# Retention queries and keys by seven block products, and weight sums by accumulating loads

## The chip, the cores and the metric

The kernel runs on one core of a Trainium2 chip. The metric is device time in microseconds of one execution. TensorE multiplies, VectorE and ScalarE read the products out of the PSUM banks and prepare operands, GpSimd does masks and small powers, and the queue of SyncE issues the transfers between DRAM and on-chip memory.

## The reference

Two layers on a 1024 x 1024 input. Layer 0 is a retention of four heads; layer 1 is a stick-breaking attention of eight heads whose keys and values come from the output of layer 0. The change touches the projections of layer 0:

```
u = rms_norm(h, ret_norm_pre[i])
proj = u @ ret_w_in[i]
q, k, v, g = split(proj)            # per head: q, k of 256 columns, v, g of 512
q = rope(q, pos)                    # [x1 cos - x2 sin, x1 sin + x2 cos]
k = rope(k, pos) * 256 ** -0.5
o = retention_chunkwise(q, k, v)
o = (o - mean(o)) * rsqrt(var(o) + EPS)
o = o * silu(g)
y = o @ ret_w_out[i]
```

## The kernel before

The sequence is worked in two halves of 512 columns (t = 0, 1): retention of both halves (phases A0 and A1), then attention of both (C0 and C1). A retention phase goes through its four heads (u = 0 to 3), an attention phase through four pairs of heads.

**Numbers as two parts.** Every operand of a matmul is held as a rounded part and a remainder. `split` (L574) makes them: ScalarE writes the rounded part (L577, L580 with a scale), VectorE the difference (L578, L581). `mm3` (L412) then issues three matmuls per product (L415, L416, L417) into one PSUM bank.

**A head of the retention** has three stages on TensorE:

- *Queries and keys*, `AHead.qk` (L730) by `proj` (L457): four units of weights of 128 x 1024; four banks (two `ma`, two `mb`), each the output of one block of 128 columns of q or k, and 96 matmuls that stream 512 columns. When the last k-tiles are through, `rope` (L715, operations L717 to L722) turns two banks at a time with twelve VectorE operations and four splits over all, into the tile `qk`, of which there is one buffer.
- *The output of the head before*, `outproj` (L484): 16 chunks of 6 matmuls. Its sides are the scores of the new head, `scores` (L869), and statistics.
- *Values and gates*, `AHead.vg` (L770): seven block products instead of eight. Its quadrants are the two halves of the 512 time columns, the two halves of the 1024 inputs, and values against gates. The sums of inputs that it needs are made once per phase, by `sums` in `a_prep` (L630), and kept as `X.T`. The sums of weights are made by VectorE in `left` (L777): additions and subtractions at L797, L800, L803 and L806 on tiles `wraw` and `S`, then split into `whl`. The products go in the order 1, 2, 5, 6, 3, 7, 4, each in two units; products 6 and 7 add to the banks of 1, and 3 to those of 5. `copy` (L821, ScalarE) and `plus` (L825, VectorE) read partial results out, `vput` (L742) and `gput` (L746) finish values and gates.

The first head of A0 does it in another way (`first_v`, `qk`, `first_g`) and keeps that.

**What sets the order.** The program is emitted as chunks: `merge` (L524) weaves side steps into the chunks of a stage, each with a number of chunks to leave free at its start and end. `run` (L1531 to L1546 for the retention) says which sides go where: the rest of the mixing and the gate of the head before go into the query/key stage, the scores into the output stage, the first mixing steps into the value/gate stage. For the last head (u = 3) the first 4 of 16 output chunks go ahead of values and gates, and 12 after. Then `arrange` (L101) orders every engine's queue anew: from a duration for each instruction (`_time`, L68), the number of buffers of each tile (`BUFS`, L319) and a model of the DMA queue, it plans the program by latest start times five times over (`place`, `justify`) and fixes the order of each queue to that of the best plan.

**Buffers** that matter here: `whl` 3 (split weights), `wraw` 6 (raw weights, 128 x 512), `S` 2 (128 x 1024, the sums), `f2` 6, PSUM banks `ma`, `mb`, `z`, `o` 2 each. `raw_w` (L342) hands out `wraw` tiles, and in attention, by `rings`, also tiles of other names. All transfers are issued by SyncE through `dma` (L359).

## Time and profile before

| | |
|---|---|
| three runs | 1715.91, 1716.36, 3299.96 us; median 1716.36 |
| the profiled execution | 1716.91 us, span 1714.8 us |
| granted TensorE clock | 0.997 |
| instructions of TensorE | 8057 matmuls and as many weight loads |
| DMA | 348.78 MB, mean 203 GB/s |

The third run is a single slow execution. In the profile, `PE` is TensorE's matmuls and `PEld` its weight loads, `DVE` is VectorE, `ACT` ScalarE, `POOL` GpSimd, `SP` SyncE. A group of instructions is listed as its line, engine and operation, output tile and input tiles, shape and count, then busy microseconds and mean nanoseconds of one, then the idle time before it and what ended it. A row of the windows gives for each engine the busy time and the number of instructions, then the granted clock, the busy share of the DMA engines and their GB/s. A row of waits gives the waiting line, the releaser, the total, the count and the longest. A row of the chain gives start, length and what ran.

### The profile page before, as it was taken

To read this page: it belongs to the slowest core of one execution; us is meant where nothing else is said; L and a number is where in the kernel's file an instruction comes from. 1 tells how busy PE (TensorE), PEld (TensorE's weight loads), DVE (VectorE), ACT (ScalarE), POOL (GpSimd) and SP (SyncE) were. 2 spreads that over 40 slices of the span, in tenths; PEclk is the share of its full clock that TensorE was granted. 3 is DMA by queue.
4 is the path that set the end of the run, shared out by engine and by line. 5 is a ranking of instruction groups with operands and counts; after the bars stand their busy time and mean duration, and the time that the engine had idled before them with its cause. 6 is when DMAs were issued, how large, how long until landed. Compare 5 with 4: busy or idle time off the path is not lost.

```text
span 1714.8 us, 23975 instructions
## 1 busy us (share of the span) xinstructions
PE 1700.1 (99%) x8057; PEld 1419.0 (83%) x8057; DVE 1308.4 (76%) x2213; ACT 880.9 (51%) x1646; POOL 142.8 (8%) x275
## 2 busy tenths in 40 slices
PE   9999999999999999999999999999999999999997
PEld 7888888888888888878888888888888888888887
DVE  8856868889867978688888778667887756656865
ACT  6435536555545535355655544544674445445643
POOL 0000101010010000101010100000001001001001
PEclk9999999999999999999999999999999999999999
DMA  5236475668545676376896999667883763463523
GB/s 187 98 105 203 148 236 185 203 193 271 187 146 176 225 240 209 98 256 209 291 320 198 332 314 308 209 209 257 280 292 111 252 225 101 160 219 99 162 95 125
DMA packets 182250, 348.78 MB, mean 203 GB/s; under 512 B 20208, under 2 KB 24432, under 8 KB 182128
## 3 DMA queue, kind: packets, MB, share of 16 engines
q1 hardware_dynamic: 182128, 347.26, 61.0%
q8 instruction: 63, 1.03, 0.2%
q14 instruction: 59, 0.48, 0.1%
HBM read 273.78 MB, written 73.40 MB: 202 GB/s over the span
## 4 chain that ended last, share of the span: by engine, by line
PE 99%; DMA 0%; DVE 0%; ACT 0%; issue 0%; SPq 0%; POOL 0%; DVEq 0%
PE pmb L415 13%; PE pmb L417 13%; PE pmb L416 13%; PE pma L415 12%; PE pma L417 12%; PE pma L416 12%; PE po L417 5%; PE po L416 5%; PE po L415 5%; PE pz L1355 2%; PE pz L417 2%; PE pz L416 2%; PE pz L415 2%; PE pz L983 1%; PE pz L551 0%; DMA S<-in_xT_dram 0%
## 5 line engine op out<-in xcount | busy, mean ns | idle before, releaser
L577 ACT ACTIVATE whl<-wraw 128x512 fp32r<-128x512 f32 x323 | 190.8, 625 | 203.4 <-PE pmb L417 80.4
L578 DVE TENSOR_TENSOR whl<-wraw,whl 128x512 fp32r<-128x512 f32 x323 | 214.3, 686 | 64.3 <-ACT whl L577 63.1
L415 PE MATMUL pma<-xh,whl 128*128 128x512 f32 x384 | 153.1, 399 | 0.0
L415 PE MATMUL pmb<-xh,whl 128*128 128x512 f32 x384 | 152.4, 397 | 0.0
L417 PE MATMUL pma<-xh,whl 128*128 128x512 f32 x384 | 150.1, 391 | 0.0
L417 PE MATMUL pmb<-xh,whl 128*128 128x512 f32 x384 | 150.0, 391 | 0.0
L416 PE MATMUL pma<-xh,whl 128*128 128x512 f32 x384 | 149.9, 390 | 0.0
L416 PE MATMUL pmb<-xh,whl 128*128 128x512 f32 x384 | 149.6, 390 | 0.0
L1325 DVE TENSOR_TENSOR_SCAN sgn<-sgn 128x384 f32<-128x384 f32 (+4 forms) x64 | 86.5, 1354 | 27.7 <-POOL sgn L1323 27.7
L580 ACT ACTIVATE whl<-wraw,gn 128x256 fp32r<-128x256 f32 (+1 forms) x144 | 80.4, 600 | 50.0 <-PE pmb L417 32.4
L577 ACT ACTIVATE AT<-pz 128x512 fp32r<-128x512 f32 (+1 forms) x96 | 46.3, 487 | 108.0 <-PE pz L1355 105.9
L1322 POOL TENSOR_SCALAR_AFFINE_SELECT A<-A 128x128 f32<-128x128 f32 x64 | 33.1, 516 | 775.1 <-ACT A L1317 775.1
L578 DVE TENSOR_TENSOR AT<-pz,AT 128x512 fp32r<-128x512 f32 (+1 forms) x96 | 52.9, 555 | 57.6 <-ACT AT L577 57.1
L581 DVE SCALAR_TENSOR_TENSOR whl<-wraw,gn,whl 128x256 fp32r<-128x256 f32 (+1 forms) x144 | 82.0, 601 | 17.1 <-ACT whl L580 16.5
L415 PE MATMUL pmb<-oT,whl 128*128 128x512 f32 x240 | 94.9, 396 | 0.0
L417 PE MATMUL pmb<-oT,whl 128*128 128x512 f32 x240 | 93.8, 391 | 0.0
L416 PE MATMUL pmb<-oT,whl 128*128 128x512 f32 x240 | 93.7, 391 | 0.0
L577 ACT ACTIVATE whl<-S 128x512 fp32r<-128x512 f32 x104 | 63.0, 628 | 48.1 <-PE pmb L417 12.5
L417 PEld LDWEIGHTS pmb<-xh,whl 128*128 128x128 f32 x384 | 72.1, 188 | 15.8
L417 PEld LDWEIGHTS pma<-xh,whl 128*128 128x128 f32 x384 | 72.1, 188 | 15.6
L416 PEld LDWEIGHTS pmb<-xh,whl 128*128 128x128 f32 x384 | 72.2, 188 | 13.5
L415 PEld LDWEIGHTS pmb<-xh,whl 128*128 128x128 f32 x384 | 72.2, 188 | 13.4
(389 smaller groups left out, 4614.0 us busy)
## 6 DMA issues: line engine op xcount, KB each, us to landing
wraw<-in_wts_dram SPq DMA_DIRECT2D x522, 256.0 KB, 3.6
y<-f SPq DMA_DIRECT2D x120, 256.0 KB, 3.2
f<-y SPq DMA_DIRECT2D x88, 256.0 KB, 4.1
S<-in_wts_dram SPq DMA_DIRECT2D x44, 256.0 KB, 4.1
vo<-in_wts_dram SPq DMA_DIRECT2D x42, 256.0 KB, 4.3
ko<-in_wts_dram SPq DMA_DIRECT2D x40, 256.0 KB, 4.4
T<-AT SPq DMA_DIRECT2D x32, 256.0 KB, 4.7
sc<-T SPq DMA_DIRECT2D x16, 512.0 KB, 5.1
```

Source lines behind the costliest of these rows:

```text
L415: MM(p, lh, rh, start=start, stop=False, **kw)
L416: MM(p, lh, rl, start=False, stop=False, **kw)
L417: MM(p, ll, rh, start=False, stop=stop, **kw)
L577: A_.activation(dst[0], src, AF.Copy)
L578: V.tensor_tensor(dst[1], src, f32(dst[0]), ALU.subtract)
L580: A_.activation(dst[0], src, AF.Copy, scale=scale)
L581: V.scalar_tensor_tensor(dst[1], src, scale, f32(dst[0]), ALU.mult, ALU.subtract)
L983: nc.tensor.transpose(pt[:, 128 * e:128 * e + 128], on[:, 128 * e:128 * e + 128], ident[:])
L1322: first = G.affine_select(a[:, dg], a[:, dg], [[-1, 128]], ALU.is_gt, 0.0, base=0, channel_multiplier=1)
L1325: V.tensor_tensor_scan(n[:, :W][:, ::-1], n[:, :W][:, ::-1], n[:, :W][:, ::-1], 1.0, ALU.mult, ALU.bypass)
L1355: nc.tensor.transpose(p[:, 128 * tb:128 * tb + 128], self.A[hh][tb][:, c0:c0 + 128], ident[:])
```

## The change

1. Queries and keys of all heads but the first of A0 are made by seven block products too. Quadrants are the two time halves of 256 columns, the two halves of the inputs, and q against k. A product has 24 matmuls that stream 256 columns, its two blocks of 128 output columns side by side in one bank. Block b of a product's bank is the b-th 128 columns of q (`m` 0) or of k (`m` 1), so the four `put`s each rotate one time half of q or of k: q's second half after product 2, k's first after 7, k's second after 4, q's first after 3. The weights are laid out in quadrants on the host (`_quads`), and a copy for the first head is appended.
2. Sums of weights, for queries and keys and for values and gates, are no longer made by VectorE: a second transfer, issued by GpSimd, adds into the tile that the first filled. Where a difference was needed, the signs of the sums of inputs and of the gate are turned, and `outproj` subtracts.
3. Values and gates go in the order 5, 1, 2, 6, 7, 3, 4.
4. `wraw` has 4 buffers for 6, `S` 3 for 2. For the last head 8 output chunks go ahead of values and gates instead of 4, and their banks are the usual ones.
5. The planner knows transfers of GpSimd, and orders reads of one bank by two engines.

```
-    BUFS = dict(xh=8, tab=2, wraw=6, whl=3, S=2, ...
+    BUFS = dict(xh=8, tab=2, wraw=4, whl=3, S=3, ...
...
+    def plus_dma(dst, src):
+        nc.gpsimd.dma_start(dst, src, accum_op=ALU.add)
...
-            V.tensor_tensor(a[:, 0], q[0], q[1], ALU.subtract)
-            V.tensor_tensor(a[:, 1], q[2], a[:, 0], ALU.subtract)
+            V.tensor_tensor(a[:, 0], q[1], q[0], ALU.subtract)
+            V.scalar_tensor_tensor(a[:, 1], a[:, 0], -1.0, q[2], ALU.mult, ALU.subtract)
...
+        def qk7(self):
+            X, quads = self.X, self.base if self.h else 128
+            box = {}
+            order = (1, 2, 5, 6, 7, 4, 3)
+            def left(n):
+                w = S("whl", [2, 1024], F32R)
+                if n == 5:
+                    box["S"] = S("S", [1024])
+                for j in range(2):
+                    cl = slice(512 * j, 512 * j + 512)
+                    src = box["S"][:, cl] if n in (5, 6, 3) else raw_w()
+                    b11, b12, b21, b22 = [wts[quads + i, :, cl] for i in range(4)]
+                    parts = {1: (b11,), 2: (b21,), 5: (b12, b22), 6: (b11,), 3: (b21,), 7: (b11, b12), 4: (b22,)}[n]
+                    for i, b in enumerate(parts):
+                        (dma if i == 0 and n not in (6, 3) else plus_dma)(src, b)
+                    split((w[:, 0, cl], w[:, 1, cl]), src)
+                return w
...
+            def put(m, half, p, c):
+                if (m, half) == (0, 1):
+                    q = self.qkt = S("qk", [4, 2, 512], F32R)
+                    self.q, self.k = [q[:, 0], q[:, 1]], [q[:, 2], q[:, 3]]
+                tl = slice(256 * half, 256 * half + 256)
+                cos, sin = [z[:, tl].unsqueeze(1).broadcast_to([128, 2, 256]) for z in (X.cos, X.sin)]
+                V.tensor_tensor(c[:], p[:], c[:], ALU.add)
+                x = c[:].rearrange("p (b t) -> p b t", b=2)
+                r, y = S("f2", [2, 256]), S("f2", [2, 256])
+                V.tensor_tensor(r[:], x, cos, ALU.mult)
+                V.tensor_tensor(y[:], x, sin, ALU.mult)
+                if m:
+                    V.tensor_tensor(r[:, 0], y[:, 1], r[:, 0], ALU.subtract)
+                    V.scalar_tensor_tensor(r[:, 1], r[:, 1], -1.0, y[:, 0], ALU.mult, ALU.subtract)
+                else:
+                    V.tensor_tensor(r[:, 0], r[:, 0], y[:, 1], ALU.subtract)
+                    V.tensor_tensor(r[:, 1], r[:, 1], y[:, 0], ALU.add)
+                res = self.qkt[:, 2 * m:2 * m + 2]
+                split((res[:, :, 0, tl], res[:, :, 1, tl]), r[:])
...
+            def chunk(n, kt):
...
+                    first = {1: "ma", 2: "ma", 5: "mb", 4: "mb"}.get(n)
+                    if first:
+                        box["p", n] = PS(first)
+                w, p = box["w"], box["p", {6: 1, 7: 1, 3: 5}.get(n, n)]
+                fresh = n in (1, 2, 5, 4)
+                xh, xl = right(n, kt)
+                for b in range(2):
+                    nl = slice(256 * kt + 128 * b, 256 * kt + 128 * b + 128)
+                    mm3(p[:, 256 * b:256 * b + 256], w[:, 0, nl], w[:, 1, nl], xh, xl, fresh and kt == b == 0, kt == 3, goes_on=not fresh or b == 1)
+                if kt < 3:
+                    return
+                if n in (1, 5, 6, 7):
+                    box[n] = copy(p)
+                if n == 2:
+                    put(0, 1, p, box[1])
+                elif n == 3:
+                    put(0, 0, p, box[6])
+                elif n == 7:
+                    put(1, 0, p, box[5])
+                elif n == 4:
+                    put(1, 1, p, box[7])
...
                     elif n == 5:
-                        a, b, src = load(1, i), load(1, 2 + i), s
-                        V.tensor_tensor(src, a, b, ALU.add)
+                        dma(src, at(1, i))
+                        plus_dma(src, at(1, 2 + i))
                     elif n == 6:
-                        a, src = load(0, i), s
-                        V.tensor_tensor(src, src, a, ALU.subtract)
+                        plus_dma(src, at(0, i))
                     elif n == 3:
-                        src = load(0, 2 + i)
-                        V.tensor_tensor(src, src, s, ALU.subtract)
+                        plus_dma(src, at(0, 2 + i))
                     elif n == 7:
-                        a, src = load(1, 2 + i), s
-                        V.tensor_tensor(src, a, src, ALU.subtract)
+                        dma(src, at(0, i))
+                        plus_dma(src, at(1, i))
...
-            order = [(n, i) for n in (1, 2, 5, 6, 3, 7, 4) for i in range(2)]
+            order = [(n, i) for n in (5, 1, 2, 6, 7, 3, 4) for i in range(2)]
...
-                        first = {1: "ma", 2: "o", 5: "mb", 4: "mb"}.get(n)
+                        first = {5: "ma", 1: "mb", 2: "o", 4: "mb"}.get(n)
...
-                        held = last.out(yd, None, None if u < 3 else ("ma",) * 4)
-                        go(held if u < 3 else held[:4],
+                        held = last.out(yd, None, None if u < 3 else None)
+                        go(held if u < 3 else held[:8],
```

In the planner, a transfer holds the queue of its issuer for 400 ns (SyncE) or 1100 ns (GpSimd) and lands 1550 or 3100 ns after its turn on the rings.

More of the change, by code (lines that the diff above doesn't have):

```diff
@@ L119, in arrange @@
         for name, m in reads:
-            s.before |= {o.k for o, n, w in last[name] if w and n & m}
+            s.before |= {o.k for o, n, w in last[name] if n & m and (w or name in banks and o.eng != s.eng)}
             s.behind |= set([o.k for o, n, w in last[name] if not w and n & m and o.eng == s.eng][-1:])
@@ L137, in arrange @@
         s.busy, s.whole = _time(s, chip)
-        s.shares = s.eng == "Pool" or s.eng == "DVE" and sum(b.tensor.name not in banks for b in s.ins) > 1
+        s.shares = s.eng == "Pool" and not s.moves or s.eng == "DVE" and sum(b.tensor.name not in banks for b in s.ins) > 1
         steps.append(s)
@@ L202, in justify @@
         line = taken[s.eng]
-        busy = max(s.busy, 400.0) if s.eng == "SP" else s.busy
+        busy = HOLD[s.eng] if s.moves else s.busy
         i = bisect.bisect(line, (t, t))
@@ L276, in place @@
         busy, whole = s.busy, s.whole
-        if e == "SP":
-            ring_free = max(t + 1000.0, ring_free) + busy * 1.05
-            end, busy = ring_free + 1550.0, 400.0
+        if s.moves:
+            ring_free = max(t + 600.0 + HOLD[e], ring_free) + busy * 1.05
+            end, busy = ring_free + (3100.0 if e == "Pool" else 1550.0), HOLD[e]
         else:
@@ L482, in proj, with outproj @@
         return Chunks([lambda j=j: chunk(j) for j in range(16)], lambda: get(0))
-    def outproj(base, oT, y_d, first, acc=None, tags=None):
+    def outproj(base, oT, y_d, first, acc=None, tags=None, turned=lambda: False):
         box = {}
@@ L1636 @@
                   _out_units(so[b:b + 512])]
+    units.append(_quads(np.concatenate([wi[:, 0:256], wi[:, 1024:1280]], axis=1)))
     gains = np.stack([np.asarray(g).reshape(8, 128) for g in
```

69 lines of the change are left out of this document (46 added, 23 removed).

## The prediction

> **What bounds the kernel now.** I read the page first, then the waits of TensorE, then the chain of waits in narrow windows, for the spacing of matmuls.
>
> ```profile
> span 1714.8 us, 23975 instructions
> PE 1700.1 (99%) x8057; PEld 1419.0 (83%) x8057; DVE 1308.4 (76%) x2213; ACT 880.9 (51%) x1646; POOL 142.8 (8%) x275
> PE 99%; DMA 0%; DVE 0%; ACT 0%; issue 0%; SPq 0%; POOL 0%; DVEq 0%
> q1 hardware_dynamic: 182128, 347.26, 61.0%
> ```
>
> The chain that ended last is TensorE for 99% of the span. Its waits by releaser, all of them over the execution:
>
> ```profile
> PE pz L415 <- ACT qk L577: 1.8, 1, 1.8
> PE pz L388 <- DVE f L386: 1.7, 1, 1.7
> PE pma L415 <- ACT oT L580: 1.2, 1, 1.2
> PE pz L1464 <- POOL col L1458: 1.0, 1, 1.0
> PE pz L1454 <- DVE acc L1447: 0.9, 1, 0.9
> ```
>
> Five waits, 6.6 us together; only the first lies in the part that changes. So the time is the number of matmuls times their spacing, and a gain comes from matmul columns alone: work taken off VectorE (76% busy) buys nothing by itself. The spacing is the distance between starts in the chain, not the duration in the list of groups, which overlaps its neighbours. A run of 128x512 matmuls, then the 128x256 matmuls of the last output projection:
>
> ```profile
> 99.96 0.23 PE pma L416
> ...
> 103.82 0.22 PE pz L983 x2
> ```
> ```profile
> 1689.91 0.12 PE pmb L417
> ...
> 1693.15 0.12 PE pma L417
> ```
>
> 17 steps in 3.86 us are 0.227 us each; 27 steps in 3.24 us are 0.120 us each. Half the columns cost 0.53 of the time.
>
> **The change part by part.** Seven query/key projections change form (heads 1 to 3 of the first half, all four of the second).
>
> *Matmuls.* Before, one takes 4 units x 2 x 4 blocks x 3 = 96 matmuls of 512 columns: 96 x 0.227 = 21.8 us. After, 7 products x 4 k-tiles x 2 blocks x 3 = 168 matmuls of 256 columns: 168 x 0.120 = 20.2 us. Saved 1.64 us each, **11.5 us** in all; one part in eight of the columns, less 72 more matmuls' fixed share. Values and gates keep their matmuls; only their order changes. By the Trainium skill (TensorE: Matmul & The Clock Gate, Back-to-back issue gap) a stream of load-and-multiply pairs runs at about 81 ns for 128 columns and 131 ns for 512; an estimate between them is 98 ns for 256, and by it the change would lose 3.9 us a projection, 27 us in all. This trace has 227 and 120 ns for the same things, so the sum goes by the rows.
>
> *The wait that goes.* The one wait in the changed part is that of the scores of the last head:
>
> ```profile
> 729.00:735.70 6.70, 4.88 (x18) 3.61 (x17) 6.70 (x12) 3.73 (x7) 0.00 (x0) 0.87 0.66 229
> 735.70:739.20 3.50, 3.50 (x13) 2.87 (x13) 1.51 (x3) 0.00 (x0) 0.41 (x1) 0.76 0.89 259
> ```
>
> TensorE lacks 1.82 us of the first stretch, and the granted clock falls to 0.87 and 0.76 in the two (0.13 x 6.7 + 0.24 x 3.5 = 1.7 us): 3.5 us. VectorE is full (6.70 of 6.70): it turns four blocks through the 12 rotary operations and 4 splits, all issued at the end. After the change three quarters of this lies earlier in the projection, and eight output chunks instead of four stand between it and the scores (4 x 6 x 0.227 = 5.4 us more cover). I take the whole **3.5 us** as gained; the ends are 0 and 3.5. What is late next is nothing on the list above.
>
> *VectorE and ScalarE.*
>
> ```profile
> L577 ACT ACTIVATE whl<-wraw 128x512 fp32r<-128x512 f32 x323 | 190.8, 625 | 203.4 <-PE pmb L417 80.4
> L578 DVE TENSOR_TENSOR whl<-wraw,whl 128x512 fp32r<-128x512 f32 x323 | 214.3, 686 | 64.3 <-ACT whl L577 63.1
> L797 DVE TENSOR_TENSOR S<-wraw,wraw 128x512 f32<-128x512 f32 x28 | 19.1, 686 | 11.7 <-DMA wraw<-in_wts_dram 11.6
> L825 DVE TENSOR_TENSOR f<-pmb,f 128x512 f32<-128x512 f32 x28 | 18.9, 683 | 1.3 <-PE pmb L417 1.3
> L722 DVE TENSOR_TENSOR f<-f,f 128x512 f32<-128x512 f32 x16 | 10.9, 680 | 0.0
> L578 DVE TENSOR_TENSOR AT<-pz,AT 128x256 fp32r<-128x256 f32 x16 | 6.7, 421 | 9.2 <-ACT AT L577 9.1
> L581 DVE SCALAR_TENSOR_TENSOR whl<-wraw,gn,whl 128x256 fp32r<-128x256 f32 x78 | 34.0, 479 | 4.4 <-ACT whl L580 4.4
> ```
> ```profile
> 183.70:212.00 28.30, 28.30 (x134) 23.45 (x133) 21.48 (x40) 14.09 (x25) 3.86 (x9) 1.00 0.47 159
> 212.00:246.00 34.00, 34.00 (x172) 28.61 (x171) 23.08 (x44) 11.97 (x22) 3.02 (x5) 1.00 0.63 212
> 246.00:286.20 40.20, 40.20 (x178) 33.30 (x178) 36.25 (x60) 25.96 (x45) 1.93 (x3) 1.00 0.64 207
> 592.70:623.80 31.10, 31.10 (x146) 25.78 (x146) 23.31 (x43) 10.70 (x18) 4.58 (x9) 1.00 0.59 202
> 623.80:649.50 25.70, 25.70 (x121) 21.62 (x121) 19.22 (x33) 8.56 (x16) 2.08 (x4) 1.00 0.69 236
> 649.50:693.20 43.70, 43.70 (x198) 36.27 (x197) 38.40 (x65) 26.53 (x47) 2.61 (x5) 1.00 0.62 199
> ```
>
> The six stretches are query/key, output and value/gate stage of a head of each half; the third number after PE and PEld is VectorE's. Value/gate loses 16 additions of 0.686: 11.0 us. Query/key gains 14 - 8 = 6 weight splits (4.1 us), and four puts of 0.68 + 2 x 0.68 + 0.42 + 0.48 + 0.69 = 3.63 (14.5 us) replace 16 operations of 0.68 (10.9 us): 7.7 us more. That stage then wants 21.5 + 7.7 = 29.2 us of VectorE in 28.3 - 1.6 = 26.7 us of TensorE (31.0 in 29.5 in the other half). The surplus of about 2 us is hidden if the last put may slip into the output stage, where VectorE has 10.9 and 6.5 us free and the scores come only after five chunks (6.8 us). I take **0**; uncovered it is 2 us x 7 = 14. ScalarE has half its time free everywhere. One wait is new: q and k have one buffer, and q's second half is put after product 2 of 7 rather than at the end, while in the second half of the sequence the head before still reads its own q in the mixing woven into this stage. The put's last two operations stand in ScalarE's and VectorE's queues until that mixing is through; the scores that need them come a stage later, so this too is 0, and without that room it is part of the 14.
>
> *The accumulating loads.* Per head 24 loads that add into a tile, issued by GpSimd, which the trace does not show. Nearest rows, a plain load and GpSimd's and SP's holds:
>
> ```profile
> S<-in_wts_dram SPq DMA_DIRECT2D x44, 256.0 KB, 4.1
> ```
> ```profile
> L555 POOL TENSOR_TENSOR col<-small,mhalf 128x4 f32<-128x4 f32 x8 | 11.3, 1408 | 110.5 <-DVE small L553 110.5
> ```
> ```profile
> L360 SPq DMA_DIRECT2D wraw<-in_wts_dram x10: 327/332/333, 1263.8 to 1278.9; - x10
> ```
>
> Landing: 4.1 us if adding is free, 8.2 if it costs a second load; issue: 0.33 to 1.41 us. They matter at one place: in the new projection product 6 follows 5, and 6's weights are 5's tile after the split and two accumulations. From the split of 5 to the weights of 6: issue, landing, two splits (2.0 us): 6.7 us at the low end, 1.41 x 2 + 8.2 + 2.0 = 13.0 at the high one. Three split buffers let 5 be split by some 2.6 us (two halves of 0.63 + 0.69) after product 1 starts, so TensorE has three products (3 x 24 x 0.120 = 8.6) less 2.6, plus the mixing woven in (21 x 0.227 = 4.8 in the first half, 33 x 0.227 = 7.5 in the second, none in its first head): 10.8, 13.5 and 6.0 us. Costs: 0.7 to 3 x 2.2 + 7.0 = 13.6 us. I take **1.5**, nearer the low end, since the row is that of a load into the same tile. Behind a waiting load on GpSimd stand the causal masks of the scores and the small powers of the normalisation; both feed work that is a chunk or more away from TensorE's need.
>
> *Products 6 and 7 on one bank.* ScalarE must copy product 6 before 7 adds to it.
>
> ```profile
> L821 ACT ACTIVATE f<-pma 128x512 f32<-128x512 f32 x42 | 24.7, 590 | 11.4 <-PE pma L417 11.1
> ```
> ```profile
> 1686.75 0.28 PE L416 MATMUL pma<-qk,xh 128*128 128x256 f32 x1
> ```
>
> Drain 0.28 - 0.12 and copy 0.59: 0.75 us, filled by product 4 or woven work where its weights are there; for values the other bank's three matmuls (0.68) fill nearly all. Ends 0 and 7 x 0.8 = 5.6; I take **1.5**, as woven work stands in most heads.
>
> *Load buffers 6 to 4.* The densest stage with this ring alone is the shared values of the last half:
>
> ```profile
> 1246.80:1278.70 31.90, 31.90 (x145) 26.56 (x144) 25.66 (x34) 24.47 (x46) 2.56 (x6) 1.00 0.92 302
> ```
> ```profile
> DMA to landing us min/median/max: 3.2/4.1/5.5
> ```
>
> 20 loads; a slot is held 0.33 + 4.1 + 1.4 = 5.9 us, so four slots pass 20 in 29.4 us of 31.9; with 1 us of waiting, 34.4. Ends 0 and 5; I take **1.0**.
>
> Signs carried through and the two half-width subtractions of the input sums cost nothing: they ride on operations that stay. **Sum**, against the profiled execution's own 1716.91 us (0.55 above the median): 1716.9 - 11.5 - 3.5 + 1.5 + 1.5 + 1.0 = **1705.9 us**, 0.64% less.
>
> **The rivals.**
> 1. *The accumulate chain shows* (13.0 us from split to weights): 1705.9 - 1.5 + 13.6 = 1718 us. For it: the first head of the second half has no cover. Against: 4.1 us for a load into this tile.
> 2. *VectorE becomes the bound of the query/key stage*, its put late and the scores waiting: 1705.9 + 14 = 1720 us. For it: 29.2 in 26.7, and the old wait was of this kind. Against: free time right behind, and a head as a whole loses 3.3 us of VectorE.
> 3. *Slower than before: the DMA engines become the bound of the retention.* A plain load's 128 packets take 0.61 x 1714.8 x 16 / 182128 = 92 ns each, 0.735 us of all 16 engines. A head's engines are busy 60 us in the first half (0.47 x 28.3 + 0.63 x 34 + 0.64 x 40.2) and 63 in the second; it loses 10 plain loads (7.4 us) and gets 24 accumulating ones. If one costs k plain ones, the need is 53.0 + 17.6k of 100.9 us, and 55.9 + 17.6k of 98.9. At k = 2 that is 0.88 and 0.92, the share at which the window above ran without a wait; it decides from k = 2.4. At k = 3: 5.1 us x 3 + 9.9 x 4 = 55 us, 1761 us. Against: an addition reads two operands and writes one, k near 2. The Trainium skill (Collectives: The Full Stack, The bandwidth ceiling) says the same: an adding transfer reads two sources and gets half the rate. No run here shows it yet.
> 4. *The narrow matmul does not keep 0.120 us* because weights bind:
>
> ```profile
> L417 PEld LDWEIGHTS pma<-qk,xh 128*128 128x128 f32 x21 | 4.0, 192 | 0.0
> ```
>
> A load lasts 192 ns there; if loads could not overlap, 7 x 168 x 0.072 = 85 us come on top, 1791 us, and the change would not do what it says. Against: those same loads ran at 0.120. This is the direction of the skill's spacing rule above.
>
> **How the numbers follow.** Forecast 0.68, rivals 0.12, 0.10, 0.08 and 0.02. With every new cost at zero the time is 1701.9; 1176 matmuls at 1 ns less give 1700, the low end. The high end takes in rivals 1 and 2 and a little of both: 1724. About 2% (34 us) is what a measurement of this kernel can tell from no change; slower by more is most of rivals 3 and 4 (0.07), faster by more none of the cases, as TensorE's columns do not give 34 us (0.01). Within 2%: 0.92.
>
> **What would show it.** Right: 168 matmuls a projection 0.120 us apart; no wait of the scores near the end of the second half's retention; TensorE's waits still under 12 us; VectorE's additions into S gone and its share down by some 20 us. Wrong: TensorE waiting for the copies or splits of query/key weights behind an accumulating load (rival 1), for the put of q and k (2), a DMA share above 0.9 through the retention with loads landing late (3), or spacing well above 0.120 (4).

## The result, and the profile after

The changed kernel takes 1764.16 us in the median (1763.45 to 1768.92), the kernel before 1715.91 beside it: a ratio of 1.0289, with a 95% interval of 1.0266 to 1.0312 (ratios are taken over the single executions, not from the two medians). Medians leave out one far slower execution each of the kernel before and of the experiments e9, e12 and e15; with it they are 1716.13, 1727.6, 1719.8 and 1712.0, and the expectations quoted below name e9 by its 1727.6. The changed kernel is 48 us slower, where 1705.9 with a range of 1700 to 1724 was forecast. The profiled execution took 1768.92 us, its span is 1767.2.

The page of the changed kernel, the lines that answer to those of before, and the one for the loads that GpSimd issues (median us to landing at its end):

```profile
span 1767.2 us, 25359 instructions
PE 1711.0 (97%) x8561; PEld 1444.9 (82%) x8561; DVE 1290.2 (73%) x2199; ACT 916.0 (52%) x1716; POOL 294.6 (17%) x443
q1 hardware_dynamic: 172048, 328.91, 55.7%
q0 software_dynamic: 24192, 44.05, 15.0%
PE 78%; DMA 10%; issue 5%; DVE 4%; ACT 2%; POOL 1%; SPq 0%; POOLq 0%; DVEq 0%; ACTq 0%
S<-in_wts_dram POOLq DMA_DIRECT2D x126, 256.0 KB, 6.4
```

The chain that ended last was TensorE for 99%; now 22% of it is something else, and the largest of that is transfers. TensorE's waits say where (us in total, times, longest):

```profile
PE pmb L420 <- ACT f L909: 17.6, 5, 4.6
PE pma L420 <- ACT whl L584: 6.2, 2, 5.4
PE po L420 <- ACT sgn L1040: 5.8, 3, 3.7
PE pmb L420 <- ACT whl L584: 5.5, 4, 3.0
PE pma L420 <- ACT f L799: 2.9, 2, 1.8
```

With the smaller rows they are 47.6 us, against 6.6 before. L909 is ScalarE's copy of a product in values and gates, L799 the same in the new projection, L584 a split of weights, L1040 ScalarE's step in the normalisation of the mixing's output. To the waits come stretches at half clock, eight of 3.4 or 6.8 us in the trace's record of the clock ahead of the one at its end, each beginning in a wait or within 1.4 us behind one. The first of them (a row of the windows, as in the prediction; the 0.50 is the granted clock), then the mean clock of the changed kernel and of the one before:

```profile
166.31:173.13 6.82, 6.06 (x14) 4.78 (x15) 1.99 (x3) 3.26 (x8) 1.23 (x2) 0.50 0.81 219
```
```profile
core 0: 1767.2 us, clock 0.986
```
```profile
core 0: 1714.8 us, clock 0.997
```

Unrounded, the two clocks are 0.98645 and 0.99668. So 0.01355 x 1767.2 = 23.9 us were lost to the clock, against 0.00332 x 1714.8 = 5.7. Then 41.0 us more waits and 18.2 more of slow clock, less the 11.5 of matmuls, make 47.7 of the 52.4 us by which the span grew. Some 4 us of that are counted twice, as 8.1 us of the half-clock stretches lie within waits; what else the span grew by was not followed.

**One wait followed to its start.** The values/gates stage of the second head, where TensorE stops for 4.2 us. The chain of waits in that window (start, length, what):

```profile
153.74 3.63 issue
157.39 0.86 POOL wraw L366
158.25 0.42 issue
158.69 7.19 DMA wraw<-in_wts_dram
166.10 0.34 issue
166.44 0.59 ACT f L909
167.07 0.79 PE pmb L420
```

Read it from the end: TensorE waited for the copy of product 6; the copy for its turn behind a split on ScalarE; the split for an accumulating load that landed at 158.69 + 7.19 = 165.88; and that load, with GpSimd's queue before it, for 3.63 us of "issue" in which no instruction is named. ScalarE's timeline shows the middle part:

```profile
162.48 0.63 ACT L584 ACTIVATE whl<-wraw 128x512 fp32r<-128x512 f32 x1 [2.77 <-DMA wraw<-in_wts_dram]
165.90 0.63 ACT L584 ACTIVATE whl<-wraw 128x512 fp32r<-128x512 f32 x1 [2.79 <-DMA wraw<-in_wts_dram]
166.44 1.07 ACT L909 ACTIVATE f<-pmb 128x512 f32<-128x512 f32 x2
```

The bank is full from 162.7 us on (its last matmul starts at 162.34 and takes 0.39); ScalarE sits still for 2.79 us, with the copy behind a split of product 7's weights in its queue. GpSimd's timeline shows the part called issue:

```profile
151.02 0.89 POOL L366 DMA_DIRECT2D wraw<-in_wts_dram  x1 [12.34 <-DVE whl L585]
152.09 0.87 POOL L366 DMA_DIRECT2D wraw<-in_wts_dram  x1 [0.18 <-issue]
153.65 0.86 POOL L366 DMA_DIRECT2D S<-in_wts_dram  x1 [0.69 <-DVE whl L585]
157.39 0.86 POOL L366 DMA_DIRECT2D wraw<-in_wts_dram  x1 [2.87 <-issue]
158.69 0.89 POOL L366 DMA_DIRECT2D wraw<-in_wts_dram  x1 [0.43 <-issue]
160.00 0.88 POOL L366 DMA_DIRECT2D S<-in_wts_dram  x1 [0.42 <-DVE whl L585]
```

The loads issued at 151.02, 152.09 and 153.65 landed at 157.08, 158.38 and 159.69. The fourth starts at 157.39, the fifth at 158.69, the sixth at 160.00: each 0.31 us after one has landed. Of the 168 accumulating loads of this execution none was issued with more than two others under way; 85 were issued with just two, 60 of them 0.26 to 0.32 us after a landing. That made the first theory: **accumulating loads are late, because only three fit at once in the store for transfer descriptors whose size the kernel sets (`dynamic_dma_scratch_size`), and the order of work was planned as if nothing limited them.**

**A second queue.** The powers of the normalisation stand on GpSimd too. The waits of ScalarE for them, the changed kernel first, then a run in which GpSimd issues no load (e8 below):

```profile
ACT sgn L1040 <- POOL small L1028: 29.6, 13, 6.4
```
```profile
ACT sgn L1040 <- POOL small L1028: 1.0, 3, 0.5
```

Three loads were under way at 531 us (issued at 526.43, 528.35 and 529.04); the next was issued at 533.07, 0.31 us after the first of them had landed. It held the last of those small products until 533.69, ScalarE's L1040 until 534.24 and TensorE until 535.07: the 3.7 us of the row PE po.

### The profile page after: what moved, and what is told of

Read it like the earlier page. It is cut to its first block, busy times and chain, and to the rows that moved or that the text cites. A ratio compares the mean times of both kernels' runs of the same rounds, so it can differ in the third digit from the quotient of the medians.

```text
span 1767.2 us, 25359 instructions
## 1 busy us (share of the span) xinstructions
PE 1711.0 (97%) x8561; PEld 1444.9 (82%) x8561; DVE 1290.2 (73%) x2199; ACT 916.0 (52%) x1716; POOL 294.6 (17%) x443
## 3 DMA queue, kind: packets, MB, share of 16 engines
q0 software_dynamic: 24192, 44.05, 15.0%
## 4 chain that ended last, share of the span: by engine, by line
PE 78%; DMA 10%; issue 5%; DVE 4%; ACT 2%; POOL 1%; SPq 0%; POOLq 0%; DVEq 0%; ACTq 0%
PE pmb L420 10%; PE pmb L422 10%; PE pmb L421 10%; PE pma L420 10%; PE pma L422 9%; PE pma L421 9%; DMA wraw<-in_wts_dram 6%; PE po L420 4%; PE po L422 4%; PE po L421 4%; DMA S<-in_wts_dram 2%; PE pz L1443 2%; DVE whl L585 2%; PE pz L422 1%; PE pz L421 1%
## 5 line engine op out<-in xcount | busy, mean ns | idle before, releaser
L584 ACT ACTIVATE whl<-wraw 128x512 fp32r<-128x512 f32 x322 | 192.8, 625 | 171.2 <-DMA wraw<-in_wts_dram 69.5
L366 POOL DMA_DIRECT2D S<-in_wts_dram x126 | 115.4, 959 | 300.2 <-DVE whl L585 146.1
L585 DVE TENSOR_TENSOR whl<-S,whl 128x512 fp32r<-128x512 f32 x146 | 97.5, 691 | 60.9 <-ACT whl L584 60.2
L420 PE MATMUL pma<-xh,whl 128*128 128x512 f32 (+1 forms) x384 | 140.2, 365 | 0.0
L422 PE MATMUL pma<-xh,whl 128*128 128x512 f32 (+1 forms) x384 | 138.1, 360 | 0.0
L421 PE MATMUL pma<-xh,whl 128*128 128x512 f32 (+1 forms) x384 | 137.9, 359 | 0.0
L584 ACT ACTIVATE whl<-S 128x512 fp32r<-128x512 f32 x146 | 87.0, 627 | 76.4 <-PE pmb L422 33.1
L420 PE MATMUL pmb<-xh,whl 128*128 128x512 f32 (+1 forms) x328 | 124.0, 379 | 0.0
L422 PE MATMUL pmb<-xh,whl 128*128 128x512 f32 (+1 forms) x328 | 122.4, 373 | 0.5 <-DVE whl L585 0.5
L421 PE MATMUL pmb<-xh,whl 128*128 128x512 f32 (+1 forms) x328 | 122.0, 372 | 0.0
L1413 DVE TENSOR_TENSOR_SCAN sgn<-sgn 128x128 f32<-128x128 f32 (+3 forms) x64 | 86.7, 1357 | 24.8 <-POOL sgn L1411 24.7
L420 PE MATMUL pmb<-oT,whl 128*128 128x512 f32 x256 | 101.4, 396 | 0.0
L584 ACT ACTIVATE AT<-pz 128x512 fp32r<-128x512 f32 (+1 forms) x96 | 46.3, 487 | 105.2 <-PE pz L1443 103.1
L421 PE MATMUL pmb<-oT,whl 128*128 128x512 f32 x256 | 100.2, 392 | 0.0
L422 PE MATMUL pmb<-oT,whl 128*128 128x512 f32 x256 | 100.0, 390 | 0.0
L585 DVE TENSOR_TENSOR AT<-pz,AT 128x512 fp32r<-128x512 f32 (+1 forms) x96 | 52.7, 554 | 59.5 <-ACT AT L584 58.5
L422 PEld LDWEIGHTS pma<-xh,whl 128*128 128x128 f32 x384 | 72.5, 189 | 11.2
L421 PEld LDWEIGHTS pma<-xh,whl 128*128 128x128 f32 x384 | 72.7, 189 | 9.5
```

Of the source, the lines that this page charges most:

```text
L366: nc.gpsimd.dma_start(dst, src, accum_op=ALU.add)
L420: MM(p, lh, rh, start=start, stop=False, **kw)
L421: MM(p, lh, rl, start=False, stop=False, **kw)
L422: MM(p, ll, rh, start=False, stop=stop, **kw)
L584: A_.activation(dst[0], src, AF.Copy)
L585: V.tensor_tensor(dst[1], src, f32(dst[0]), ALU.subtract)
```

## The experiments

The times are medians, each with its ratio to the kernel before, run beside it (1715.6 to 1716.6 us in every set).

| run | us | ratio, 95% interval |
|---|---|---|
| changed kernel | 1764.2 | 1.0289 [1.0266, 1.0312] |
| e1: descriptor store 2048 for 1024 bytes | 1736.0 | 1.0117 [1.0100, 1.0134] |
| e2: sums by VectorE | 1746.5 | 1.0176 [1.0158, 1.0194] |
| e3: values and gates alone changed | 1752.8 | 1.0210 [1.0195, 1.0225] |
| e4: products 3 and 7 exchanged | 1752.0 | 1.0208 [1.0190, 1.0227] |
| e5: store 2048 and a plan that knows of it | 1728.7 | 1.0078 [1.0057, 1.0098] |
| e6: the plan alone, store 1024 | 1734.8 | 1.0115 [1.0095, 1.0134] |
| e7: plain loads by GpSimd, no sums | 1707.4 | 0.9957 [0.9941, 0.9974] |
| e8: plain loads by SyncE, no sums | 1704.6 | 0.9938 [0.9923, 0.9953] |
| e9: queries and keys alone changed | 1726.5 | 1.0071 [1.0051, 1.0091] |
| e10: e9 with store and plan | 1725.0 | 1.0056 [1.0041, 1.0071] |
| e11: e9 with all sums by VectorE | 1743.1 | 1.0163 [1.0148, 1.0179] |
| e12: e5 with 3 and 7 exchanged | 1719.2 | 1.0026 [1.0014, 1.0037] |
| e13: e9 with six load buffers | 1717.4 | 1.0012 [1.0002, 1.0021] |
| e14: e13 with store and plan | 1714.7 | 0.9994 [0.9985, 1.0003] |
| e15: e13 with plain loads, no query/key sums | 1711.6 | 0.9977 [0.9967, 0.9987] |
| e16: e8 with every such transfer twice | 1704.0 | 0.9933 [0.9916, 0.9950] |

### Is it the accumulating loads at all? (e7, e8)

```diff
-        nc.gpsimd.dma_start(dst, src, accum_op=ALU.add)
+        nc.gpsimd.dma_start(dst, src)
```


> The changed kernel with GpSimd's transfers plain, so that the second block of weights overwrites the first and no sum is made. Theory A: without a second operand to read, a load takes about half the descriptors, so five or more are on their way; they land in 4 to 5.5 us and the time is 1710 to 1730 us. If it is GpSimd's issuing and not the adding (theory G), three at a time remain and the time is 1750 us or more.

```diff
-        nc.gpsimd.dma_start(dst, src, accum_op=ALU.add)
+        dma(dst, src)
```


> The changed kernel with those transfers plain and issued by SyncE, so that no sum is made and nothing accumulates: seven products, their order, the same bytes and the smaller raw-weight ring are left. If the whole loss is the accumulating loads', 1700 to 1712 us (the prediction's sum without its 1.5 for them is 1704.4); if products, buffers or VectorE's query/key stage cost too, 1718 us or more.

1707.4 and 1704.6 us, the first a little below the range of theory A, the second within the range for the loads. With plain loads in the same places (the last load then stands for the sum), all else of the change is there: the seven products, the new order, four load buffers, two products on one bank, the turned signs. All of TensorE's waits in e8:

```profile
PE pz L393 <- DVE f L391: 1.7, 1, 1.7
PE pz L1552 <- POOL col L1546: 1.0, 1, 1.0
PE pz L1542 <- DVE acc L1535: 0.9, 1, 0.9
PE pma L420 <- ACT qk L584: 0.8, 1, 0.8
PE pma L420 <- ACT oT L587: 0.6, 1, 0.6
PE pma L421 <- DVE qk L585: 0.3, 1, 0.3
```

5.3 us, and none of a microsecond in the part that changed. So 1764.2 - 1704.6 = **59.5 us are the accumulating loads**. e8 was planned anew, as its loads stand in SyncE's queue; in e7 the order of every queue is that of the changed kernel, and nothing but the adding is gone: 1764.2 - 1707.4 = 56.7 us. The 2.8 us between e7 and e8 are what issuing by GpSimd costs for plain loads, the other plan included. e7 also gives the price of the adding to the DMA engines:

```profile
q0 software_dynamic: 13440, 44.05, 7.6%
S<-in_wts_dram POOLq DMA_DIRECT2D x126, 256.0 KB, 4.6
```

The same 44.05 MB in 168 plain loads: 0.076 x 1705.6 = 130 us of all 16 engines, against 0.150 x 1767.2 = 265 with the adding, 2.04 times; landing 4.6 against 6.4 us.

### Room for the descriptors, and the plan (e1, e5, e6)

```diff
-... dynamic_dma_scratch_size=1024)
+... dynamic_dma_scratch_size=2048)
```


> The changed kernel with GpSimd's store for transfer descriptors at 2048 bytes a partition instead of 1024; every queue keeps its order. Theory A (store full: in the changed kernel never more than three accumulating loads are on their way, and the fourth is issued 0.3 us after the oldest lands): five to seven may be under way, GpSimd's unexplained idle time before its transfers (56 us) goes, TensorE's waits fall from 45 us to under 15 and the time to 1705 to 1722 us. Theory B (an accumulating load of 6.4 us is simply too slow for the order that was planned): the waits stay above 35 us, 1755 to 1766 us.

1736.0 us, 28.1 less, with the order on every queue unchanged. GpSimd's timeline at the same place as above:

```profile
151.80 0.86 POOL L366 DMA_DIRECT2D wraw<-in_wts_dram  x1 [12.37 <-DVE whl L585]
153.25 0.86 POOL L366 DMA_DIRECT2D wraw<-in_wts_dram  x1 [0.58 <-DMA wraw<-in_wts_dram]
154.40 0.86 POOL L366 DMA_DIRECT2D S<-in_wts_dram  x1 [0.29 <-DVE whl L585]
155.17 1.90 POOL L366 DMA_DIRECT2D wraw<-in_wts_dram  x2
156.46 3.29 POOL L366 DMA_DIRECT2D S<-in_wts_dram  x3
```

Eight loads are issued between 151.8 and 159.8 us, where the changed kernel had issued five by then, and up to seven are under way. That each now takes longer to land (7.0 us in the median) doesn't undo it: the wait for the copies of L909 falls from 17.6 to 6.0 us. TensorE's waits fall from 47.6 to 25.0 us. So neither theory has it: B's waits above 35 us are gone, A's under 15 did not come. The limit of three is shown, and with this order of work it costs 28 us.

```diff
+CAP = 7
...
-        return n * 512 / 330.0, 4000.0 if s.eng == "SP" else 6000.0
+        return n * 512 / 330.0 * (1.0 if s.eng == "SP" else 1.9), 4000.0 if s.eng == "SP" else 6000.0
...
+            if e == "Pool" and len(fly) >= CAP:
+                t = max(t, fly[-CAP] + 300.0)
...
+            if e == "Pool":
+                fly.append(end)
```
With the store of 2048 bytes:

> The store at 2048 bytes and a planner that knows better: an accumulating load holds the rings 1.9 times as long as a plain one (175 against 92 ns a packet in the changed kernel's profile) and no more than seven are on their way. Theory P (what is left at 1736 us is an order planned on landings that are too early): TensorE's waits under 12 us, 1705 to 1720 us. Theory L (the latency itself does not fit the buffers): 1726 to 1740 us.

With CAP = 3 and the store of 1024:

> The changed kernel with the store left at 1024 bytes, the planner knowing the 1.9 and that only three accumulating loads are on their way at once. Theory A in its strict form (three at a time are too few for this work): 1740 us or more. If the order alone was wrong (theory P alone), 1705 to 1725 us.

1728.7 and 1734.8 us. e5 is in the range of theory L, with 19.6 us of TensorE's waits where theory P wanted under 12. e6 lies between what the two theories gave: with three under way, a plan that knows the limit gets 29.3 us back, as much as the room alone. The two don't add (35.4 together): they mend the same lateness, one by shortening it, the other by putting work ahead of it.

### ScalarE's queue (e4, e12)

```diff
-            order = [(n, i) for n in (5, 1, 2, 6, 7, 3, 4) for i in range(2)]
+            order = [(n, i) for n in (5, 1, 2, 6, 3, 7, 4) for i in range(2)]
...
-                        first = {5: "ma", 1: "mb", 2: "o", 4: "mb"}.get(n)
+                        first = {5: "ma", 1: "mb", 2: "o", 4: "ma"}.get(n)
```


> The changed kernel with values and gates in the order 5, 1, 2, 6, 3, 7, 4, so that product 7 does not follow 6 onto the same banks. Theory D (one bank for neighbours is the cause, the loads being late only by accident): 1735 us or less. Theories A and B: the waits move to the split of 7's weights instead of the copy of 6, 1750 to 1770 us.

1752.0 us: 12 us better, no cure. The copy is no longer due while the next product's weights are awaited, and the wait goes to the split itself; the first row of TensorE's waits is now

```profile
PE pma L420 <- ACT whl L584: 18.3, 13, 2.8
```

So ScalarE's queue is where the lateness showed, and the weights are late whoever waits for them. With store and plan as in e5:

> The changed kernel with the store of 2048 bytes and the planner's 1.9 and seven under way (which gave 1728.7 us), and products 3 and 7 of values and gates exchanged (5, 1, 2, 6, 3, 7, 4), so that no copy of a bank is due while the weights of the product right behind it are awaited. Theory A with the order (the 20 us of waits that are left stand at the turn from 6 to 7, where ScalarE's queue holds the copy behind a split): 1712 to 1720 us. Theory P (what is left is at the turn of the halves and at the change to attention, where the plan has too little room ahead of it): 1725 to 1735 us, as without the exchange.

1719.2 us, 9.5 below e5 and at the upper end of what theory A gave: the exchange keeps most of its worth behind the other two repairs. Theory A's place for e5's waits is not borne out, though: none of e5's 19.6 us is for the copies of values and gates, and one wait, of 3.6 us, is for such a copy in the new projection.

### Sums by VectorE instead (e2, e11)

```diff
-        nc.gpsimd.dma_start(dst, src, accum_op=ALU.add)
+        t = raw_w()
+        dma(t, src)
+        V.tensor_tensor(dst, dst, t, ALU.add)
```


> The changed kernel with each accumulating load made a plain load by SyncE and an addition by VectorE; seven products, their order and all buffers as in the change. Theories A and B both blame the accumulating loads and expect the waits on them gone: 1705 to 1725 us, with VectorE 16.5 us a head busier. Theory C (the seven products themselves, by VectorE's load in the query/key stage, are what stalls): 1745 us or more.

1746.5 us, a miss for whoever expected the loss to vanish with the accumulating loads, and theory C's time. The waits go over to VectorE and its neighbours, the longest rows of e2:

```profile
PE pz L578 <- DVE sgn L571: 5.1, 1, 5.1
PE pma L422 <- ACT f L801: 3.9, 2, 2.1
```

That VectorE has no room for 24 additions a head in this order (16 in the kernel before) is the likely reading, not a shown one: each of these additions also takes one more of the four load buffers, and e2 does not part the two. e11 is the same with the values and gates in their old order:

> As the first run of this set, but with the sums of the query/key weights too made by VectorE after plain loads by SyncE: no accumulating load anywhere. It adds 8 additions of 0.686 us to a query/key stage that by the prediction wants 29.2 us of VectorE in 26.7 (31.0 in 29.5 in the second half): 34.7 in 26.7. Theory V (VectorE then bounds that stage, and the earlier run with all sums on VectorE lost its 42 us there): 1730 to 1750 us. Theory O (that run lost its time to values and gates, whose new order 5, 1, 2, 6, 7 asks for the sums at once and early): 1705 to 1718 us.

1743.1 us: theory V by the time, 16.6 above e9. Between the first and the last matmul of the seven projections TensorE waits 12.5 us, against 3.3 in e9, mostly for mixing, normalisation and input sums that stand in VectorE's and ScalarE's queues. But VectorE isn't full there: but for the first head of the second half (26.4 us busy of 28.1) the stages stretch to 34 to 38 us with 27 to 31 us of it busy, where the theory counted 34.7 in 26.7. That the additions make the loss is shown; whether by VectorE's time or by the load buffers that they take isn't, as e11 was not run with six buffers.

### Which part of the change? (e3, e9, e10, e13, e14, e15)

e3 undoes the new projection, and with it the 8 output chunks ahead of the last head's values and gates (4 again), and keeps the accumulating loads and the new order in values and gates:

```diff
-                        go(H.qk7())
+                        go(H.qk())
...
-        units += [_quads(qk) if h else _in_units(qk),
+        units += [_in_units(qk),
```


> Accumulating loads and the new order for values and gates, queries and keys by eight products as before. If values and gates' sixteen accumulating loads are the place (theories A and B; five of the waits there are 17.6 us), most of the loss is here too: 1740 to 1765 us. If the projection's own accumulations cost (rival 1 of the prediction), 1716 to 1725 us.

1752.8 us, 36 more than the kernel before. Two rows of TensorE's waits:

```profile
PE pmb L420 <- ACT f L909: 16.1, 5, 4.2
...
PE pz L420 <- ACT qk L584: 1.8, 1, 1.8
```

The first is the longest row of the changed kernel again (17.6 there), made by values and gates alone. The second is the wait of the scores in the last head, which comes back with the old projection. The two parts do not simply add, though: with the 11.5 + 3.5 us that the new projection should save, e3 would give 1737.8 us, and the changed kernel is 26.4 above that.

e9 does the other part alone: the new projection with its 8 accumulating loads a head, and values and gates in the old order with sums by VectorE.

```diff
-            order = [(n, i) for n in (5, 1, 2, 6, 7, 3, 4) for i in range(2)]
+            order = [(n, i) for n in (1, 2, 5, 6, 3, 7, 4) for i in range(2)]
...
-                        plus_dma(src, at(1, 2 + i))
...
+                        V.tensor_tensor(src, x, y, ALU.add)
```


> Queries and keys of the heads in seven products with their accumulating loads, as in the changed kernel; values and gates go back to the order 1, 2, 5, 6, 3, 7, 4 with their weight sums by VectorE, and keep the changed signs (so 8 accumulating loads a head, of 24). Theory A (the loss is made by accumulating loads that want more than three under way at once, and that happens in values and gates, where 16 of the 24 stand): 1704 to 1715 us, TensorE's waits under 15 us. Theory R1 (rival 1 of the prediction: the chain from product 5's split through two accumulating loads to product 6's weights shows in the query/key projection): 1715 to 1730 us, with TensorE waiting for the splits of query/key weights, 2 us and more at each of the seven. Theory S (losses of the two parts add; the run with values and gates alone accumulated left 22 of the 59.5 us to queries and keys): 1727 us.

> As the run before it, with a descriptor store of 2048 bytes for 1024 and the planner told that an accumulating load holds the DMA engines 1.9 times as long as a plain one and that seven may be under way. Theory A: 1704 to 1710 us, faster than the kernel before by 0.3 to 0.7%, and the fastest of all kernels that compute the reference. Theory R1: the chain of two accumulating loads is no longer for lack of room and the plan knows its length, so still 1712 to 1725 us where no other work can be put under it.

1726.5 and 1725.0 us. Theory A, which put nearly all of the loss in values and gates, is wrong on both; 1727 was theory S's number. Theory R1's ranges hold both, but not its sign: a wait of 2 us and more for query/key weights stands in one of the seven projections, not in each. Of e9's 12.4 us of waits in the parts that change, 9.0 stand in values and gates again, at splits behind VectorE's sums, and those sums take two of the four load buffers at once. So the buffers were put back:

```diff
-    BUFS = dict(xh=8, tab=2, wraw=4, whl=3, S=3, ...
+    BUFS = dict(xh=8, tab=2, wraw=6, whl=3, S=2, ...
```


> The query/key projections alone in seven products with accumulating loads, values and gates in the old order with sums by VectorE (the run that gave 1727.6 us), now with the load buffers as in the kernel before: wraw 6 and S 2 for 4 and 3. Theory B (of the 23 us that this arrangement lost, most are the two buffers': values and gates take two of them for one sum of VectorE, and the copies then stand behind splits that wait for that sum): 1706 to 1715 us. Theory R1 (they are the chain of accumulating loads in the query/key projection): 1720 to 1729 us, as before.

> The same with the store of 2048 bytes and the planner's 1.9 and seven under way. Theory B: 1703 to 1710 us, faster than the kernel before by 0.3 to 0.7%. Theory R1: 1715 to 1725 us.

> The first of this set with the query/key accumulating loads as plain loads by SyncE into the same places, so that the query/key weight sums are not made (the last load stands for the sum); values and gates are complete. Theory B: 1703 to 1708 us, and within 8 us of the run with accumulating loads. Theory R1: 1703 to 1708 us too, but 15 us and more below it. Over 1712 us, the loss is neither's but that of the old values and gates beside the new projection.

1717.4, 1714.7 and 1711.6 us. The buffers were 9.1 us of e9, and e13's distance to e15, 1717.41 - 1711.55 = **5.9 us**, is the price in this arrangement of the accumulating loads in the query/key projection, all eight a head: theory B's bound of 8 us holds but its times of 1706 to 1715 and 1703 to 1710 do not, and R1 (15 us and more) has it no better. Of TensorE's rows, the two longest of e13, then the longest of e15:

```profile
PE pma L420 <- DVE f L522: 4.1, 2, 3.1
PE pma L420 <- ACT whl L584: 3.2, 1, 3.2
```
```profile
PE pma L420 <- ACT whl L584: 2.8, 1, 2.8
```

The long ones stand in the first head of the second half, the head without cover (at 424 and 437 us in e13, at 432 in e15). The waits at 437 and 432 are for the same weights, those of product 6, so nearly all of that one is there without an accumulating load. In all, TensorE's waits are 13.5 us in e13 and 11.5 in e15, the time at half clock 20.4 and 12.7 us. e15 isn't at e8's 1704.6: 6.9 us remain in this arrangement with no accumulating load in it, and they were not taken further. e14 is the fastest kernel here that makes all the sums, and it can't be told from the kernel before (0.9994, 0.9985 to 1.0003); no version was found that beats it.

### The engines' time (e16)

What is left is rival 3's mechanism: an accumulating load takes the DMA engines twice as long. Around the wait shown first, the stretch 160 to 168 us of the changed kernel (busy us of PE, PEld, DVE, ACT and POOL, then granted clock, DMA share, GB/s):

```profile
160.00:168.00 8.00, 3.79 (x17) 3.03 (x16) 2.01 (x3) 2.73 (x6) 2.60 (x3) 0.89 0.98 209
```

The engines are full there. e16 takes e8 and sends every such block a second time, by SyncE, to a place in device memory that nothing reads:

```diff
-        nc.gpsimd.dma_start(dst, src, accum_op=ALU.add)
+        dma(dst, src)
+        turns_idle[0] += 1
+        dma(idle[turns_idle[0] % 8][:], src)
```


> The run whose 168 replaced loads were plain loads by SyncE (no weight sums made; 1704.6 us, 59.5 below the changed kernel), and behind each of them a second transfer of the same 256 KB by SyncE into a buffer in device memory that nothing reads: about the engines' time of accumulating loads (2.0 plain loads each), without GpSimd, its descriptor store or the adding. Theory E (rival 3 as far as it is local: the engines' time of the second pass is what makes the weights late, the share was 0.9 to 0.98 beside the waits): 1725 to 1745 us, as the accumulating loads with a store of 2048 bytes (1736.0), with TensorE waiting for splits and copies in values and gates. Theory A (the engines have room for it; the loss is the latency of the accumulating load, its place in GpSimd's order and the three under way): 1704 to 1712 us. In between, the distance from 1704.6 is the engines' part.

1704.0 us: theory A. The stretch from 100 to 300 us, in e16 and then in the changed kernel:

```profile
100.00:300.00 200.00, 200.00 (x1093) 173.49 (x1091) 143.07 (x257) 112.08 (x203) 18.03 (x33) 1.00 0.93 316
```
```profile
100.00:300.00 200.00, 189.24 (x970) 161.06 (x969) 129.79 (x228) 102.01 (x184) 48.37 (x65) 0.97 0.79 202
```

Engines that are 93% busy leave TensorE without a gap; at 79% with accumulating loads it lacks 10.8 us. The loads that are waited for land in 4.2 (`wraw`) and 4.8 us (`S`) in the median of e16, 3.7 and 4.2 in e8. So full engines beside a wait do not by themselves make it. The limit of this test: nothing waits for the second transfer, so it shows that the engines' time is there, not that a load with two passes could land as early as a plain one.

## Why the prediction was wrong, point by point

**The step that failed** is the term of 1.5 us for the accumulating loads, and in it the sentence "They matter at one place". It measures 59.5 us (56.7 with every queue's order kept, e7). The durations it was made from were bounded rightly in the middle: landing 4.1 to 8.2 us was forecast and 6.4 measured in the median (13 of the 168 took longer than 8.2, the longest 10.4), issue 0.33 to 1.41 and 0.86 to 0.96 measured in the mean. And the one place that was priced, from product 5 to 6 in the query/key projection, is not where the loss is: in the changed kernel all waits in the new projections are 9.6 of the 47.6 us. The longest, 5.4 us, is product 6 waiting in the head that the prediction called uncovered; 3.7 us at half clock behind it cost 1.9 more, and the 7.3 us are within the bounds of 0.7 to 13.6. What was missing:

- *Sixteen of the 24 loads a head were given no price.* They are in values and gates; the changed kernel waits there for its copies of L909 (17.6 us), and e3, which has only them, loses 36 us. The prediction left that stage at "keep their matmuls; only their order changes".
- *A resource was not counted.* The bounds were for one load by itself. How many can be under way was asked neither of the trace nor of the kernel's last lines, where the store is given 1024 bytes. Three at once, each some 6.4 us, is one load in 2.1 us at best; where the room is there, eight are issued within 8 us (e1).
- *The queues behind a late load were named incompletely.* Of GpSimd's, the masks and the powers were named and their users called "a chunk or more away": the powers cost TensorE 5.8 us. ScalarE's queue, in which the split of late weights stands ahead of the copy of a full bank, was not named at all.
- *A wait costs more than its length.* The prediction itself read 3.5 us off a wait of 1.8, and then priced the new waits without the clock: 18.2 us, some 4 of them within the waits.

**What held.** Without the failed term the prediction's sum is 1704.4 us, and e8 measures 1704.6. That they meet within 0.2 us is in part luck: the sum starts from 1716.9, and the kernel before took 1715.6 beside e8, so 10.9 us were gained where the other terms say 12.5. The terms in it stand on their rows: the new matmuls run 0.120 us apart, as in the new projection of the second head (36 starts from 188.35 to 192.54, 4.19 us for 35 steps; in the whole retention of e8, 1086 of the 1174 steps between neighbouring 256-column matmuls are 118 to 122 ns)

```profile
188.35 0.28 PE L420 MATMUL pma<-xh,whl 128*128 128x256 f32 x1
...
192.54 0.28 PE L422 MATMUL pma<-xh,whl 128*128 128x256 f32 x1
```

so rival 4 is out, and the Trainium skill's spacing rule (TensorE: Matmul & The Clock Gate, Back-to-back issue gap), by which the narrow matmuls would lose, doesn't fit this kernel; the measurement decides. The wait of the scores in the last head is in no list of the changed kernel or of e8, and is back in e3, which has the old projection (1.8 us). VectorE did not become the bound (rival 2): no wait of a microsecond is left in the changed part of e8, and in the changed kernel VectorE's busy time fell by 18.2 us, where some 20 were forecast. Whether four load buffers cost the 1.0, and the shared bank its 1.5, e8 can't tell one by one; together they fit. In another arrangement the same two buffers cost 9.1 us (e9 to e13): the term was right for these stages, not for four buffers as such.

**Rival 3** named 1761 us, 3 from the result, by luck, and is wrong as a mechanism: it needed k = 2.4 to decide and k = 3 for its price, k measures 2.04 against GpSimd's plain loads (265 / 168 = 1.58 us a load, 2.15 times the 0.735 of SyncE's), and e16 has the engines busier with no loss. The Trainium skill says that a reducing transfer reads two sources and gets half the rate (Collectives: The Full Stack, The bandwidth ceiling); the factor 2.04 bears out the half, and no run here shows that the second read is the reason. Slower by over 2% was given a chance of 0.07 because it was tied to the engines alone; a queue of limited depth is a second way to the same end.

**What stays open.** From the changed kernel the repairs go 1764.2, 1736.0 (room), 1728.7 (plan), 1719.2 (exchange). The last 14.6 us to e8 are unsettled: e16 speaks against the engines' time, within its limit, and e7 says that issuing by GpSimd isn't to blame. Later landing (7.0 against 4.6 us) is what remains by argument, and no run shows it alone. Of e5's 19.6 us of waits 10.3 stand between 329 and 458 us, around the turn of the two halves. In e12's trace 8.7 of the 16.8 us stand in the new projection, the three longest (2.6, 1.9 and 1.9 us) at product 6 waiting for the split of `S`: with the rest mended, the chain of rival 1 is the largest group among the waits that are left.

## What to carry to other kernels

Before a new kind of transfer is priced by its latency, count how many of them may be under way at once and how many a stage asks for in a row, over all places where it is used and not only at the tightest chain. Then follow each late arrival through the in-order queues, to what stands behind the waiting instruction on each engine, and add the slow clock after the stop. An order worked out from planned durations is only as good as these: telling the plan of the limit and of the longer hold gave back as much as widening the limit under the old plan (29.3 and 28.1 us of 59.5), about half each.

## What the runs showed of the hardware that was not expected

- With a descriptor store of 1024 bytes at most three accumulating loads of 256 KB were under way, with plain loads up to seven (e7); with 2048 bytes up to seven accumulating ones. At the limit the next was issued 0.3 us after one had landed (60 loads of the changed kernel), and the profile puts much of that time down as "issue", with no releaser.
- An accumulating load is 144 packets for the 80 of a plain one that GpSimd issues (24192 and 13440 in 168 loads), 2.04 times the engines' time. The bytes are counted once, so GB/s looks low where the engines are full: 209 GB/s at a share of 0.98, where plain loads give 316 at 0.92 (e16, 160 to 168 us).
- 24192 more packets of plain copies could be put into the retention with no effect on the time (e16 1704.0 us, e8 1704.6).
